# A hybrid decoder layer: norms of projection and down results dealt one token tile at a time, operands of the next products built in single steps

## The chip, the cores and the metric

The kernel runs on one core of a Trainium2 chip. The metric is the device time of one execution in microseconds (us), as the median of several runs. Beside the runs there is one profiled execution, from which every row below comes.

## The reference

One layer on 2048 tokens of width 1024, in float32. The first two lines below (projection, recurrent and attention heads) are far from the change; what matters is from `mix` on.

```python
u = rmsnorm(h, attn_pre_norm); proj = u @ w_in
o_hg, o_sb = ...                      # HGRN2 heads and stick-breaking heads, each normalised
mix = concatenate([o_hg, o_sb]) @ w_out
h = h + rmsnorm(mix, attn_post_norm)  # norm of the projection result
u = rmsnorm(h, ffn_pre_norm)
gate, up = split(u @ w_gate_up, [2816])
y = (silu(gate) * up) @ w_down
h = h + rmsnorm(y, ffn_post_norm)     # norm of the down result
h = h + (p @ ple_proj) * sigmoid(h @ ple_gate)
```

## The kernel before

Tokens are worked in four groups `g` of 512, each of four tiles of 128 rows. A float32 product is made on TensorE (PE) from three passes: an operand is split into a rounded high part (`uh`, `wh`) and the remainder (`ul`, `wl`), and `mm3` adds high by high, low by high and high by low (L221, L222, L223). The high part is a cast on ScalarE (ACT, L753), the low part a subtraction on VectorE (DVE) or GpSimd (POOL) (L754). `pair_of` (L745) makes both and is told which of the two engines subtracts: `V` is DVE, `G` is POOL.

After attention and recurrence come these stages:

- `out_proj(g)` (L611) multiplies by `w_out`; ACT (L643) and DVE (L645) bring its results into tiles `mix`. The projection of group 3 is the last and stands alone.
- `post_mix(g)` (L649) norms a group's projection result: for each token tile ACT squares (L258), POOL makes the reciprocal root (L260, L250, L252), DVE multiplies by root and gain (L660), POOL adds the residual (L661), the sum is squared and scaled in the same way, and both are stored (`h_s`, `un_s`).
- `turn` (L668) loads the normed rows, transposes them on PE and stores them as `u_s`, operands of the next product.
- Then a list of steps, run by `Drive`, two groups at a time: `gate_up(0)`, `down(0)`, `gate_up(1)`, `down(1)`, `ple(0)`, `ple(1)`. Each product of two matrices is cut into 2 by 2 blocks and made from seven block products in the order `CHAIN = (1, 2, 6, 3, 7, 5, 4)`, as in Strassen's scheme; sums and differences of blocks ("combos") are made on DVE or POOL before, and results are added together as they come (`chain`, L857). `gate_up` has 77 steps of 24 matmuls (11 blocks of the hidden width by seven products), `down` 77 steps of 12 matmuls (seven products by 11 blocks), each `ple` 36 steps.
- `t_first`, `t_second`, `t_all` build the token-side operands of the gate-and-up products from `u_s`; `s_all` and `s_one` those of the `ple` products from `h2t_s`. `post_y(g, i, ...)` (L1005) norms one token tile of a `down` result: it loads the gain twice and the residual twice, and stores two halves of `h2_s`, which a later `turn` transposes into `h2t_s`.

Loads by `load()` go out on SP's queue, all into one ring of ten tiles named `wr`, each 128 by 512 float32 (256 KB). A load is issued when the tile that it takes is free. `Drive.run` calls `prepare` of a step a fixed number of steps ahead of its matmuls: three in `gate_up` and `down`, five in `ple`. `at` and `spread` hook further work behind given steps. PE runs in the order of the program; on the other engines, and on SP, a scheduler puts the instructions in the order in which it takes them to be ready, and each engine then runs strictly in that order.

Of the kernel before, what the change touches and what calls it, by code (L numbers as in the profile page):

```python
# [18 lines left out]
ND = D // P  # L19
# [65 lines left out]
def hybrid_block(  # L85
# [563 lines left out]
    def post_mix(g, mix):  # L649
        gb = [ev(name="gb") for _ in range(2)]  # L650
        for j in range(2):
            nc.sync.dma_start(gb[j], attn_post_norm[0:1][:, j * GT:(j + 1) * GT].to_broadcast((P, GT)))
        for t in range(TT):
            hs = [xt("h"), xt("h")]
            for j in range(2):
                nc.sync.dma_start(hs[j], x[g * GT + t * P:g * GT + (t + 1) * P, j * GT:(j + 1) * GT])
            r = row_rstd(mix[t])
            for j in range(2):
                d = mix[t][j]
                nc.vector.scalar_tensor_tensor(d, d, r, gb[j], op0=ALU.mult, op1=ALU.mult)  # L660
                nc.gpsimd.tensor_tensor(hs[j], hs[j], d, op=ALU.add)  # L661
                nc.sync.dma_start(h_s[g][t * P:(t + 1) * P, j * GT:(j + 1) * GT], hs[j])
            r = row_rstd(hs)
            for j in range(2):
                nc.scalar.activation(mix[t][j], hs[j], AF.Copy, scale=r)
# [94 lines left out]
    def add(e, o, a, b):  # L760
        e.tensor_tensor(o, a, b, op=ALU.add)  # L761
# [33 lines left out]
    def t_blk(grp, i, j, k):  # L795
        return load(u_s[2 * grp + j][4 * i + k])
# [20 lines left out]

    def t_all(grp, tt, k):
        b11, b12, b21, b22 = (t_blk(grp, i, j, k) for i, j in ((0, 0), (0, 1), (1, 0), (1, 1)))
        for prod, b in ((1, b11), (2, b21), (3, b22)):  # L820
            tt[prod, k] = pair_of(b, "u", prod, V)
        b_combos(b11, b12, b21, b22, G)
        for prod, b in ((5, b11), (7, b12), (6, b22), (4, b21)):
            tt[prod, k] = pair_of(b, "u", prod, V)

    def s_blk(grp, i, j, k):
        return load(h2t_s[2 * grp + i][4 * j + k])

    def s_all(grp, ss, k):
        a11, a12, a21, a22 = (s_blk(grp, i, j, k) for i, j in ((0, 0), (0, 1), (1, 0), (1, 1)))  # L830
        for prod, a in ((1, a11), (2, a12), (4, a22)):
            ss[prod, k] = pair_of(a, "u", prod, V)
        add(G, a22, a21, a22)
        sub(G, a21, a11, a21)
        sub(G, a11, a22, a11)
        sub(G, a12, a12, a11)
        for prod, a in ((6, a11), (3, a12), (7, a21), (5, a22)):
            ss[prod, k] = pair_of(a, "u", prod, V)

    def s_one(grp, ss, prod, k):  # L840
        if prod in (1, 2, 4):
            a = s_blk(grp, *{1: (0, 0), 2: (0, 1), 4: (1, 1)}[prod], k)
        elif prod == 7:
            a, a21 = s_blk(grp, 0, 0, k), s_blk(grp, 1, 0, k)
            sub(V, a, a, a21)
        else:
            a21, a = s_blk(grp, 1, 0, k), s_blk(grp, 1, 1, k)
            add(V, a, a21, a)
            if prod != 5:
                a11 = s_blk(grp, 0, 0, k)  # L850
                sub(V, a, a, a11)
            if prod == 3:
                a12 = s_blk(grp, 0, 1, k)
                sub(V, a, a12, a)
        ss[prod, k] = pair_of(a, "u", prod, G)

    def chain(prod, c, b, new):  # L857

# [29 lines left out]
    def gate_up(grp, tt):  # L888
        def block(fb):
# [76 lines left out]
            blocks = blocks[2:]  # L966
        return steps + [b[p] for b in blocks for p in CHAIN]

    def down(grp):
        nfb = DFF // 256  # L970
        cs = [{} for _ in range(TT)]
# [2 lines left out]
        def product(n, prod):  # L974
# [12 lines left out]
            def run(k):  # L987
# [16 lines left out]
    def post_y(g, i, halves):  # L1004
# [151 lines left out]
    for g in range(NG - 1):  # L1156
# [5 lines left out]
            hgs[2].drain()  # L1162
            weave(op, OP_SLOTS - 6, rates.part(OP_SLOTS - 6), r3.part(OP_SLOTS - 6, 1))
        elif g == 1:
            weave(op, half, rates.part(half), r3.part(half, 1))
            tu = Stream(turn(un_s[0], u_s[0], g_ffn, "tr", xt, ev))
            weave(op, half, rates.part(half), r3.part(half, 1), (tu, 9, 0))
        else:
            weave(op, half, rates.part(half), r3.part(half, 1))
            hgs[3].drain()  # L1170
            att_stream.drain()
            side.close()
# [8 lines left out]
            for k in range(ND // 2):  # L1181
                t_first(0, tt0, 6, k)
        op.drain()
        post_mix(g, res[g]["mix"])
# [12 lines left out]

    def at(stage, step, f):
# [59 lines left out]
```

## Time and profile before

| quantity | value |
|---|---|
| time, median of 3 runs | 3174.49 us (3174.29 to 3177.37) |
| profiled execution: its own time | 3183.32 us |
| its span, first to last instruction | 3181.5 us |
| mean granted PE clock | 0.966 |
| busy share | PE 92%, DVE 63%, POOL 59%, ACT 50% |

Each row of a view is one group of instructions or one stretch of time. Busy shares are means over stages that differ. In rows of windows, the first number is the stretch, then its length, then busy time and count of instructions of each engine, then the granted PE clock (1.00 is full speed), the busy share of the 16 DMA engines and the GB/s that they moved. In rows of waits, the pair behind PE is what waited and what came last: total, times, longest, all in us.

### The profile page before, as it was taken

How to read it: one execution, taken by the hardware profiler on the slowest of the kernel's cores; microseconds unless marked ns; L12 is line 12 of the kernel's file. 1: busy time of each engine (PE TensorE's matmuls, PEld its weight loads, DVE VectorE, ACT ScalarE, POOL GpSimd, SP SyncE). 2: the span in 40 equal slices, each digit the busy share in tenths (PEclk: the TensorE clock that was granted, in tenths of full speed). 3: DMA queues.
4: the chain of work that ended last, by engine and by line, in shares of the span. 5: the costliest groups of instructions: out<-in, count | busy, mean ns of one | idle time of the engine just before them, and what ended most of it. 6: DMA issues, size and time to landing. Idle time of an engine off the chain costs nothing. (4 is left out here: it accounts for less than half of the span.)

```text
span 3181.5 us, 53147 instructions
## 1 busy us (share of the span) xinstructions
PE 2932.7 (92%) x18280; PEld 2455.3 (77%) x18280; DVE 1993.6 (63%) x2595; ACT 1591.3 (50%) x3187; POOL 1874.1 (59%) x1808
## 2 busy tenths in 40 slices
PE   7999899989999988778689999999799999998889
PEld 5888688868887877768568787878687888886667
DVE  3555566667776766555666666766575666655464
ACT  5666656656666665665433333355333332554342
POOL 3344445535556566665666666666756565766584
PEclk9999999999999999899789999999899999999989
DMA  6775465545545444548556676677755564677895
GB/s 186 221 209 164 135 182 162 152 131 163 160 147 156 128 141 132 169 142 287 183 187 209 229 239 219 210 218 230 265 181 178 193 211 149 210 217 252 283 317 163
DMA packets 467279, 613.32 MB, mean 193 GB/s; under 512 B 43840, under 2 KB 270144, under 8 KB 467008
## 3 DMA queue, kind: packets, MB, share of 16 engines
q1 hardware_dynamic: 467008, 609.92, 61.2%
q8 instruction: 144, 2.36, 0.3%
q14 instruction: 127, 1.04, 0.1%
HBM read 450.90 MB, written 158.86 MB: 192 GB/s over the span
## 5 line engine op out<-in xcount | busy, mean ns | idle before, releaser
L754 POOL TENSOR_TENSOR wl<-wr,wh 128x512 fp32r<-128x512 f32 x388 | 564.7, 1465 | 432.2 <-ACT wh L753 389.7
L753 ACT CAST wh<-wr 128x512 fp32r<-128x512 f32 x600 | 353.3, 620 | 565.7 <-PE mm L222 182.5
L413 POOL TENSOR_TENSOR a<-be,ring 128x512 f32<-128x512 f32 (+2 forms) x320 | 314.2, 982 | 493.9 <-DVE ring L409 462.7
L221 PE MATMUL mm<-uh,wh 128*128 128x512 f32 x1168 | 485.2, 415 | 2.2 <-DVE vv L328 1.9
L223 PE MATMUL mm<-uh,wl 128*128 128x512 f32 x1168 | 461.2, 395 | 0.0
L222 PE MATMUL mm<-ul,wh 128*128 128x512 f32 x1168 | 460.8, 394 | 0.0
L221 PE MATMUL mm<-wh,uh 128*128 128x256 f32 (+1 forms) x1024 | 322.0, 314 | 10.1 <-ACT mix L643 9.4
L754 DVE TENSOR_TENSOR wl<-wr,wh 128x512 fp32r<-128x512 f32 x212 | 222.7, 1062 | 166.1 <-ACT wh L753 153.3
L409 DVE TENSOR_TENSOR_SCAN ring<-z,ring,be 128x512 f32<-128x512 f32 x192 | 245.9, 1281 | 99.3 <-ACT z L395 94.0
L222 PE MATMUL mm<-wl,uh 128*128 128x256 f32 (+1 forms) x1024 | 305.1, 298 | 0.0
L223 PE MATMUL mm<-wh,ul 128*128 128x256 f32 (+1 forms) x1024 | 304.8, 298 | 0.0
L426 DVE TENSOR_TENSOR al<-tr,ah 128x512 fp32r<-128x512 f32 (+1 forms) x320 | 192.5, 601 | 113.4 <-ACT ah L424 112.4
L223 PEld LDWEIGHTS mm<-uh,wl 128*128 128x128 f32 x1168 | 221.9, 190 | 49.8
L221 PEld LDWEIGHTS mm<-uh,wh 128*128 128x128 f32 x1168 | 223.5, 191 | 43.8 <-issue 2.0
L207 ACT CAST wh<-wr 128x512 fp32r<-128x512 f32 x288 | 178.4, 620 | 150.3 <-PE mm L222 75.3
L222 PEld LDWEIGHTS mm<-ul,wh 128*128 128x128 f32 x1168 | 223.2, 191 | 38.9
L208 POOL TENSOR_TENSOR wl<-wr,wh 128x512 fp32r<-128x512 f32 x144 | 187.7, 1303 | 84.1 <-ACT wh L207 74.7
L394 ACT ACTIVATE be<-z 128x512 f32<-128x512 f32 (+2 forms) x320 | 171.3, 535 | 101.8 <-PE z L388 50.0
L424 ACT CAST ah<-tr 128x512 fp32r<-128x512 f32 (+1 forms) x320 | 167.7, 524 | 94.9 <-PE tr L421 91.4
L221 PEld LDWEIGHTS mm<-wh,uh 128*128 128x128 f32 x1024 | 200.8, 196 | 18.4 <-ACT mix L643 10.1
L222 PEld LDWEIGHTS mm<-wl,uh 128*128 128x128 f32 x1024 | 201.1, 196 | 5.2
L223 PEld LDWEIGHTS mm<-wh,ul 128*128 128x128 f32 x1024 | 200.5, 196 | 3.9
(288 smaller groups left out, 7363.5 us busy)
## 6 DMA issues: line engine op xcount, KB each, us to landing
wr<-in_w_gate_up_dram SPq DMA_DIRECT2D x308, 256.0 KB, 3.4
wr<-in_w_in_dram SPq DMA_DIRECT2D x224, 256.0 KB, 3.2
wr<-hid_s SPq DMA_DIRECT2D x154, 256.0 KB, 3.6
wr<-in_w_down_dram SPq DMA_DIRECT2D x110, 256.0 KB, 3.2
wr<-h_s SPq DMA_DIRECT2D x96, 256.0 KB, 4.2
hid_s<-hs SPq DMA_DIRECT2D x88, 256.0 KB, 2.9
wr<-wd_s SPq DMA_DIRECT2D x88, 256.0 KB, 4.1
kt<-k_s SPq DMA_DIRECT2D x80, 256.0 KB, 3.0
```

What stands on the lines that cost most here:

```text
L207: nc.scalar.copy(hi, src)
L208: (lo_engine or nc.gpsimd).tensor_tensor(lo, src, hi.bitcast(F32), op=ALU.subtract)
L221: nc.tensor.matmul(o, l[0], r[0], start=start, stop=False)
L222: nc.tensor.matmul(o, l[0], r[1], start=False, stop=False)
L223: nc.tensor.matmul(o, l[1], r[0], start=False, stop=stop)
L394: nc.scalar.activation(be[:, :n], z[:, :n], AF.Sigmoid, scale=0.125)
L409: nc.vector.tensor_tensor_scan(r[:, o:o + n][:, ::-1], z[:, :n][:, ::-1], be[:, :n][:, ::-1], init, op0=ALU.mult, op1=ALU.bypass)
L413: nc.gpsimd.tensor_tensor(a[:, :n], be[:, :n], r[:, o + 1:o + n + 1], op=ALU.mult)
L424: nc.scalar.copy(hi[:, lo_c:], tr[:, lo_c:])
L426: nc.vector.tensor_tensor(lo[:, lo_c:], tr[:, lo_c:], hi[:, lo_c:].bitcast(F32), op=ALU.subtract)
L753: nc.scalar.copy(hi, src)
L754: lo_engine.tensor_tensor(lo, src, hi.bitcast(F32), op=ALU.subtract)
```

## The change

Eight edits, which leave every matmul as it is:

1. `post_mix` yields behind each token tile. Those of groups 0 to 2 are woven into the next `out_proj`, one tile at a time; that of group 3 goes behind steps 0 to 3 of `gate_up(0)`, one tile each (before: all four behind step 0).
2. Behind the last `out_proj`, `prepare` runs for four steps (before: for two, ahead of that `out_proj`, as still now); the four calls of `t_second` are hooked behind steps 0 to 3 of `gate_up(0)` (before: all ahead of step 0).
3. `down` prepares four steps ahead, not three.
4. `post_y` is called per tile behind steps 67, 69, 71 and 73 of `down`, or 0 to 3 of the stage that follows (before: four tiles at once behind products 5 and 4).
5. `t_all` and `s_all` are generators, spread over nine steps for each `k`; their combos go from POOL to DVE.
6. `s_one`, one product per step with its own loads (56 in all), becomes `s_part`, two parts for each `k`, with 32 loads.
7. In `gate_up` DVE makes the low parts of the second tile of every product, and both of products 6 and 3 (before: the second tile of products 2 and 7 alone).
8. The turns of groups 2 and 3 in `ple(0)` start one step later.

```diff
@@ post_mix
                 nc.sync.dma_start(un_s[g][t * P:(t + 1) * P, j * GT:(j + 1) * GT], mix[t][j])
+            yield
@@ t_all (s_all in the same way, add and sub from G to V)
         b11, b12, b21, b22 = (t_blk(grp, i, j, k) for i, j in ((0, 0), (0, 1), (1, 0), (1, 1)))
+        yield
         for prod, b in ((1, b11), (2, b21), (3, b22)):
             tt[prod, k] = pair_of(b, "u", prod, V)
-        b_combos(b11, b12, b21, b22, G)
+            yield
+        b_combos(b11, b12, b21, b22, V)
...
-    def s_one(grp, ss, prod, k):
...
-        ss[prod, k] = pair_of(a, "u", prod, G)
+    def s_part(grp, ss, part, k):
+
+        a11, a12, a21, a22 = (s_blk(grp, i, j, k) for i, j in ((0, 0), (0, 1), (1, 0), (1, 1)))
+        if part == 0:
+            ss[1, k] = pair_of(a11, "u", 1, G)
+            ss[2, k] = pair_of(a12, "u", 2, V)
+            add(V, a21, a21, a22)
+            sub(V, a21, a21, a11)
+            ss[6, k] = pair_of(a21, "u", 6, V)
         else:
+            ss[4, k] = pair_of(a22, "u", 4, G)
+            add(V, a22, a21, a22)
+            sub(V, a21, a11, a21)
+            sub(V, a11, a22, a11)
+            sub(V, a12, a12, a11)
+            for prod, a, e in ((3, a12, V), (7, a21, V), (5, a22, G)):
+                ss[prod, k] = pair_of(a, "u", prod, e)
@@ gate_up, prepare
-                s[prod] = [pair_of(t, "w", prod, V if n and prod in (2, 7) else G) for n, t in enumerate(w)]
+                s[prod] = [pair_of(t, "w", prod, V if n or prod in (6, 3) else G) for n, t in enumerate(w)]
@@ down, run
                 if k == nfb - 1 and prod in (5, 4):
-                    for i in range(TT):
-                        half = 0 if prod == 5 else 1
-                        post_y(2 * grp + half, i, [cs[i][1 + half, 1], cs[i][1 + half, 2]])
+                    half = 0 if prod == 5 else 1
+                    ready[2 * grp + half] = [[cs[i][1 + half, 1], cs[i][1 + half, 2]] for i in range(TT)]
@@ the last projection and the steps
-    drive = Drive([(gate_up(0, tt0), 3), (down(0), 3), (gate_up(1, tt1), 3), (down(1), 3),
+        pm = Stream(post_mix(g, res[g]["mix"]))
+
+    drive = Drive([(gate_up(0, tt0), 3), (down(0), 4), (gate_up(1, tt1), 3), (down(1), 4),
                    (ple(0, ss0), 5), (ple(1, ss1), 5)])
     drive.prepare(2)
-    Stream(out_proj(NG - 1, res[NG - 1])).drain()
+    op = Stream(out_proj(NG - 1, res[NG - 1]))
+    weave(op, OP_SLOTS, (pm, TT, 0))
+    op.drain()
...
-    for k in range(ND // 2):
-        t_second(0, tt0, k)
-
+    drive.prepare(4)
...
-    at(0, 0, lambda: post_mix(NG - 1, res[NG - 1]["mix"]))
+    for k in range(ND // 2):
+        at(0, k, lambda k=k: t_second(0, tt0, k))
+    spread(0, 0, post_mix(NG - 1, res[NG - 1]["mix"]), TT)
...
-        at(1, 6 + 15 * k, lambda k=k: t_all(1, tt1, k))
+        spread(1, 3 + 18 * k, t_all(1, tt1, k), 9, 2)
         at(2, 10 + 16 * k, lambda k=k: ple_combos(k))
-        at(3, 6 + 15 * k, lambda k=k: s_all(0, ss0, k))
+        spread(3, 3 + 18 * k, s_all(0, ss0, k), 9, 2)
+    for g in range(NG):
+        stage, step = ((1, 67), (2, 0), (3, 67), (4, 0))[g]
+        for i in range(TT):
+            at(stage, step + (2 * i if g % 2 == 0 else i), lambda g=g, i=i: post_y(g, i))
...
-        spread(4, 1 + 9 * i, turner(h2_s[g], h2t_s[g], None), 9)
-    for i, prod in enumerate(CHAIN):
+        spread(4, 2 + 9 * i, turner(h2_s[g], h2t_s[g], None), 9)
+    for i in range(2):
         for k in range(ND // 2):
-            n = 12 + 4 * i + k
-            at(4 + n // 36, n % 36, lambda prod=prod, k=k: s_one(1, ss1, prod, k))
+            at(4, 21 + 7 * i + 2 * k - i * k, lambda i=i, k=k: s_part(1, ss1, i, k))
```

Two places where the order of instructions moves are shown. The first is ACT's order where the last `out_proj` ends and `gate_up(0)` begins. `mix` is the last projection result, `uh` a token-side operand of `t_second`, `wh` a weight operand of a later step, `cu` the copy of the first block product. Before:

```order
L643 ACTIVATE mix<-mm,rg 128x256 x2
L258 ACTIVATE junk,ss<-mix 128x512
L753 CAST uh<-wr 128x512 x8
L861 COPY cu<-mm 128x512
L753 CAST uh<-wr 128x512
L861 COPY cu<-z 128x512
L753 CAST uh<-wr 128x512 x7
L753 CAST wh<-wr 128x512 x6
L258 ACTIVATE junk,ss<-h 128x512 x2
```

And with the change:

```order
L643 ACTIVATE mix<-mm,rg 128x256 x2
L258 ACTIVATE junk,ss<-mix 128x512
L754 CAST wh<-wr 128x512 x2
L754 CAST uh<-wr 128x512 x4
L754 CAST wh<-wr 128x512
L869 COPY cu<-mm 128x512
L754 CAST wh<-wr 128x512 x2
L869 COPY cu<-z 128x512
L754 CAST uh<-wr 128x512 x4
L754 CAST wh<-wr 128x512
L258 ACTIVATE junk,ss<-h 128x512 x2
```

Before, all 16 `uh` of `t_second` stand ahead of the first further weights; now the weights of steps 2 to 4 stand between eight of them, and the other eight follow later.

The second is SP's order in the last product of `down(0)`, where the loads of `post_y` for group 0 stand (gain `ffn_post_norm`, residual `h_s0`, results to `h2_s0`), beside the loads of the product (`hid_s0`, `wd_s`). Before, with the last of sixteen `post_y` loads and the first loads of the product behind them:

```order
L738 DMA wr_26009<-in_ffn_post_norm_dram 128x512
L738 DMA wr_26012<-h_s0_87 128x512
L1012 DMA h2_s0_91<-c12_25322 128x512
L738 DMA wr_26016<-in_ffn_post_norm_dram 128x512
L738 DMA wr_26019<-h_s0_87 128x512
L1012 DMA h2_s0_91<-c11_24699 128x512
L738 DMA wr_26023<-hid_s0_111 128x512
L738 DMA wr_26025<-wd_s3_278 128x512
L738 DMA wr_26051<-hid_s0_111 128x512
```

And with the change, from the second of the four tiles:

```order
L739 DMA wr_26071<-in_ffn_post_norm_dram 128x512
L739 DMA wr_26074<-h_s0_87 128x512
L1022 DMA h2_s0_91<-c11_24706 128x512
L739 DMA wr_26078<-in_ffn_post_norm_dram 128x512
L739 DMA wr_26081<-h_s0_87 128x512
L1022 DMA h2_s0_91<-c12_25306 128x512
L739 DMA wr_26085<-hid_s0_111 128x512
L739 DMA wr_26087<-wd_s8_283 128x512
L739 DMA wr_26109<-hid_s0_111 128x512
L739 DMA wr_26111<-wd_s9_284 128x512
L739 DMA wr_26146<-in_ffn_post_norm_dram 128x512
```

Before, all sixteen `post_y` loads stand ahead of the product's fourth block (`wd_s3`); now four of them alternate with four loads of the product, from its fifth block or later on.

Up to the end of the second-last `out_proj`, ACT, DVE and POOL have the same order in both kernels, row for row, though `post_mix` of groups 0 and 1 is written into the loop in another way. PE's order is the same throughout but for two sets of four transposes, one step later. DVE has 198 instructions more, POOL 202 fewer, SP 24 fewer (the loads that `s_part` saves).

More of the change, by code (lines that the diff above doesn't have):

```diff
@@ L830, in s_all @@
         a11, a12, a21, a22 = (s_blk(grp, i, j, k) for i, j in ((0, 0), (0, 1), (1, 0), (1, 1)))
+        yield
         for prod, a in ((1, a11), (2, a12), (4, a22)):
             ss[prod, k] = pair_of(a, "u", prod, V)
[L833 to L836, printed above, removed]
+            yield
+        add(V, a22, a21, a22)
+        sub(V, a21, a11, a21)
+        sub(V, a11, a22, a11)
+        sub(V, a12, a12, a11)
         for prod, a in ((6, a11), (3, a12), (7, a21), (5, a22)):
             ss[prod, k] = pair_of(a, "u", prod, V)
-    def s_one(grp, ss, prod, k):
[L841 to L845, printed above, removed]
-        else:
[L847 to L854, printed above, removed]
-        ss[prod, k] = pair_of(a, "u", prod, G)
+            yield
+    def s_part(grp, ss, part, k):
[6 more added lines that the diff above has]
+            ss[6, k] = pair_of(a21, "u", 6, V)
+        else:
+            ss[4, k] = pair_of(a22, "u", 4, G)
+            add(V, a22, a21, a22)
+            sub(V, a21, a11, a21)
+            sub(V, a11, a22, a11)
+            sub(V, a12, a12, a11)
+            for prod, a, e in ((3, a12, V), (7, a21, V), (5, a22, G)):
+                ss[prod, k] = pair_of(a, "u", prod, e)
     def chain(prod, c, b, new):
@@ L967, in gate_up @@
         return steps + [b[p] for b in blocks for p in CHAIN]
+    ready = {}
     def down(grp):
@@ L995, in run, with post_y @@
                 if k == nfb - 1 and prod in (5, 4):
-                    for i in range(TT):
-                        half = 0 if prod == 5 else 1
-                        post_y(2 * grp + half, i, [cs[i][1 + half, 1], cs[i][1 + half, 2]])
+                    half = 0 if prod == 5 else 1
+                    ready[2 * grp + half] = [[cs[i][1 + half, 1], cs[i][1 + half, 2]] for i in range(TT)]
             return [(lambda k=k: prepare(k), lambda k=k: run(k)) for k in range(nfb)]
         return [st for n, prod in enumerate(CHAIN) for st in product(n, prod)]
-    def post_y(g, i, halves):
+    def post_y(g, i):
+        halves = ready[g][i]
         r = row_rstd(halves)
@@ L1164, in hybrid_block @@
         elif g == 1:
-            weave(op, half, rates.part(half), r3.part(half, 1))
+            weave(op, half, rates.part(half), r3.part(half, 1), (pm, TT, 0))
             tu = Stream(turn(un_s[0], u_s[0], g_ffn, "tr", xt, ev))
@@ L1168, in hybrid_block @@
         else:
-            weave(op, half, rates.part(half), r3.part(half, 1))
+            weave(op, half, rates.part(half), r3.part(half, 1), (pm, TT, 0))
             hgs[3].drain()
@@ L1183, in hybrid_block @@
         op.drain()
-        post_mix(g, res[g]["mix"])
-    drive = Drive([(gate_up(0, tt0), 3), (down(0), 3), (gate_up(1, tt1), 3), (down(1), 3),
+        pm = Stream(post_mix(g, res[g]["mix"]))
+    drive = Drive([(gate_up(0, tt0), 3), (down(0), 4), (gate_up(1, tt1), 3), (down(1), 4),
                    (ple(0, ss0), 5), (ple(1, ss1), 5)])
     drive.prepare(2)
-    Stream(out_proj(NG - 1, res[NG - 1])).drain()
+    op = Stream(out_proj(NG - 1, res[NG - 1]))
+    weave(op, OP_SLOTS, (pm, TT, 0))
+    op.drain()
     wpool_open.close()
```

1 line of the change is left out of this document (added).

## The prediction

> **What bounds the kernel now.** I read the engines' busy shares first:
>
> ```profile
> span 3181.5 us, 53147 instructions
> PE 2932.7 (92%) x18280; PEld 2455.3 (77%) x18280; DVE 1993.6 (63%) x2595; ACT 1591.3 (50%) x3187; POOL 1874.1 (59%) x1808
> ```
>
> PE sets the time and its matmuls do not change. So the question is where PE idles, and where its clock is halved, within reach of the edits. I read the stretches next (length, busy PE, PEld, DVE, ACT, POOL, clock, DMA share, GB/s):
>
> ```profile
> 1553.00:1625.00 72.00, 42.04 (x144) 31.10 (x143) 45.89 (x52) 35.22 (x74) 49.88 (x52) 0.72 0.69 219
> 1625.00:2010.00 385.00, 373.84 (x1671) 308.52 (x1670) 258.33 (x318) 121.25 (x211) 241.32 (x167) 0.98 0.67 218
> 2225.00:2300.00 75.00, 56.99 (x223) 44.93 (x222) 44.01 (x50) 28.74 (x62) 61.08 (x60) 0.84 0.82 274
> 2300.00:2690.00 390.00, 386.55 (x1726) 319.21 (x1726) 265.67 (x326) 125.67 (x215) 238.29 (x167) 0.99 0.57 185
> 2690.00:2890.00 200.00, 200.00 (x884) 165.42 (x883) 116.96 (x132) 98.54 (x177) 134.65 (x90) 1.00 0.67 210
> 2890.00:2960.00 70.00, 49.40 (x194) 39.29 (x193) 35.85 (x42) 28.54 (x61) 51.54 (x54) 0.83 0.81 269
> 2960.00:3100.00 140.00, 123.10 (x543) 99.16 (x542) 79.22 (x95) 60.16 (x106) 87.52 (x62) 0.93 0.89 298
> ```
>
> The fifth stretch runs at full clock without a gap: 200.00/884 = 0.226 us for a matmul. By that pace the 144 matmuls of the first stretch need 32.6 of its 72 us, so 39.4 are lost; the stretch at 2225 loses 75 − 50.4 = 24.6, at 2890 70 − 43.9 = 26.1, at 2960 140 − 122.8 = 17.2 (a little more, since some of these are short transposes). The loss is idle time plus clock: at 1553, 30 us idle (72 − 42.04) and 9 of slower matmuls, with the clock at 0.72. The whole gate-and-up stretches (1625, 2300) lose hardly anything.
>
> Then PE's waits, for the stretches from 1240, 1640, 2230, 2330 and 2910 us in this order:
>
> ```profile
> PE tr L221 <- ACT wh L753: 13.3, 1, 13.3
> PE av L221 <- ACT wh L753: 12.6, 2, 7.4
> PE mm L221 <- ACT mix L643: 9.4, 2, 8.3
> PE hg L503 <- POOL qp L540: 8.8, 2, 5.9
> PE tr L223 <- POOL wl L754: 3.7, 1, 3.7
> ...
> PE z L223 <- DVE wl L754: 1.0, 1, 1.0
> ...
> PE z L221 <- ACT wh L753: 14.7, 2, 10.2
> ...
> PE tr L223 <- POOL wl L754: 3.5, 1, 3.5
> ...
> PE z L221 <- ACT wh L753: 14.2, 2, 10.8
> PE hg L687 <- DMA wr<-h_s: 9.3, 2, 7.2
> ```
>
> The long waits are for a cast of weights on ACT, one kind at four places. What makes ACT late differs. At 2242 and 2909 on ACT, and for the first of them on SP:
>
> ```profile
> 2242.42 1.95 ACT L753 CAST wh<-wr 128x512 fp32r<-128x512 f32 x3 [12.68 <-DMA wr<-hid_s]
> ...
> 2909.74 1.94 ACT L753 CAST wh<-wr 128x512 fp32r<-128x512 f32 x3 [13.23 <-DMA wr<-hid_s]
> ...
> 2212.97 0.33 SPq L738 DMA_DIRECT2D wr<-in_ffn_post_norm_dram  x1
> ...
> 2235.27 0.45 SPq L738 DMA_DIRECT2D wr<-h_s  x1
> 2236.42 0.42 SPq L738 DMA_DIRECT2D wr<-hid_s  x1
> ```
>
> From 2212.97 to 2235.27 SP issues the sixteen loads of `post_y`; the product's next load stands behind them and goes out at 2236.42. The wait before 2909 is the same burst of group 2. At 1564 ACT is late by its order instead: its casts of weights stand behind sixteen `uh` casts of `t_second`, which wait for DVE (its idle time of 4.26 us ends with DVE's last combo):
>
> ```profile
> 1576.98 3.22 ACT L753 CAST wh<-wr 128x512 fp32r<-128x512 f32 x6 [4.26 <-DVE wr L758]
> ```
>
> **The change part by part.** The durations (count, then total us and mean ns) by group, two single operations of one form on DVE, and ACT in the last projection:
>
> ```profile
> L754 POOL TENSOR_TENSOR wl<-wr,wh 128x512 fp32r<-128x512 f32 x388 | 564.7, 1465 | 432.2 <-ACT wh L753 389.7
> L754 DVE TENSOR_TENSOR wl<-wr,wh 128x512 fp32r<-128x512 f32 x212 | 222.7, 1062 | 166.1 <-ACT wh L753 153.3
> L761 DVE TENSOR_TENSOR c<-mm,cu 128x512 f32<-128x512 f32 x74 | 50.0, 684 | 40.5 <-PE mm L223 40.1 <-DMA un_s<-mix 0.4
> ...
> 1590.44 1.78 DVE L758 TENSOR_TENSOR wr<-wr 128x512 f32<-128x512 f32 x1
> 1609.46 0.69 DVE L758 TENSOR_TENSOR wr<-wr 128x512 f32<-128x512 f32 x1
> ...
> 1521.48 1.34 ACT L665 ACTIVATE mix<-h,rstd 128x512 f32<-128x512 f32 x2 [3.16 <-POOL rstd L252]
> ```
>
> *Weaving `post_mix`* (1): groups 0 and 1 leave the engines' orders as they were, so the waits there (POOL `qp`, 8.8 us) stay: 0. In the last projection, PE's 8.3 us wait for ACT `mix` ends with ACT behind L665, which waits for POOL's root; there POOL now has one `wl` (1.465 us) fewer ahead. Gain 1.5, bounds 0 and 5.
>
> *`prepare(4)` and the dealt `t_second`* (2), between 1553 and 1625: weights for step 2 are cast ahead, and the 13.3 and 3.7 us go. What is late next is step 5 (product 6 of the second block), whose second operand DVE reaches as its 43rd instruction after the projection, behind combos of `t_second`, L660 and `chain` adds. DVE takes 45.89/52 = 0.88 us each here, so 38 us from 1553, that is 1591; by the 1.062 us of the `wl` row, 1599. PE, at 5.5 us (24 × 0.226) a step, wants it at 1553 + 27.5 + 1.4 = 1582. So 9 to 17 us of wait. DVE's waits for loads come on top of its busy time, so I take 16, with 6 for the clock (as 9 go with 30 now): 22 of the 39.4 stay, gain 17. Bounds: 35 (DVE slips in ahead) and 5 (those waits are as long as now, when 26 of DVE's 72 us are idle).
>
> *`post_y` by tiles, lead of four* (3, 4): sixteen loads and eight stores of 256 KB no longer stand in a row, yet they remain. From the start of the last product to the next stage the queue carries 14 loads of the product, 10 for `gate_up(1)`, 16 and 8 for `post_y`: 48 transfers, 12.6 MB. The stretch at 2960 has 298 GB/s at a DMA share of 0.89, so 335 at full share: 37.6 us, against 11 steps of 12 × 0.226 = 2.7, that is 30 us. So about 7.7 us of the wait stay, in pieces, and 1.4 for the clock: of 24.6 lost, 15.5 gained. Bounds 6 (as many pieces again) and 23. The group 2 burst (2890 to 2960) is alike, 7 kept; in addition the turn's wait of 9.3 us for `h_s` loads behind `post_y(3)` goes to some 3 with eight loads fewer ahead of it and a start one step later: 26.1 − 7 − 3 − 3 for clock = 13. Bounds 3 and 22.
>
> The Trainium skill, "DMA: Bandwidth & Descriptors", section "Where 436 GB/s comes from", says that transfers between HBM and SBUF are bound by the HBM side at about 358 GB/s per core. By that 12.6 MB would take 35.2 us, 5.2 kept instead of 7.7, an estimate from the page that the 335 here neither reaches nor contradicts.
>
> *Low parts to DVE* (7): seven more of the 14 in each of 22 blocks. At 1.062 us 77 more are 82 us in 390 us of `gate_up(1)`: DVE goes from 266 to 347, 89%; POOL falls by 77 × 1.465 = 113 to 126. The add with one operand outside SBUF takes 0.684, so 0.38 of the 1.062 is meeting POOL, which will be met half as often: DVE then nearer 76%. Hidden by the lead of three steps (16 us); without that cover each late low part costs its own microsecond. I set a loss of 3, bounds 0 and 26 (at the 1.78 us of the slower single one: 77 × 1.78 + 266 = 403, 13 over, twice). The 3.5 us wait for POOL `wl` at 2447, behind POOL's sums, goes: gain 3.5, bounds 0 and 5.
>
> The Trainium skill, "SBUF — State Buffer", section "SBUF: two separate sides", says that a DVE operation with two SBUF inputs and a GpSimd one that reads SBUF take the shared ports as an exclusive lock, each for its whole instruction. The two single durations, 1.78 and 0.69 us, agree with it; by that rule each moved subtraction holds the lock for 0.69 us where POOL held it for up to 1.465, and the move would leave no loss at all.
>
> *`t_all`, `s_all`* (5) lie in the `down` stages, where PE has no gap (2690: 200.00 of 200.00 us) and DVE 117 of 200 us: sixteen combos per stage added there are 17 us, 0. *`s_part`* (6): 24 loads fewer are 6.3 MB, 19 us at 335 GB/s, in a stretch at DMA share 0.89; against it steps 28 to 31 each give DVE four sums and two subtractions, 4 × 0.9 + 2 × 1.06 = 5.7 us in 2.7 of matmuls, ten steps or so ahead of most use. Of the 17.2 lost I take half as staying, since steps on DVE replace loads: gain 8, bounds −5 and 15.
>
> **Sum:** 1.5 + 17 + 15.5 + 13 + 3.5 + 8 − 3 = 55.5. The profiled execution took 3183.3 us (span 3181.5 and 1.8 around it), so 3127.8 by its own measure; the median of the runs is 8.8 lower than it, so 3174.5 − 55.5 = 3119.
>
> **Rivals.** *Half of it* (moved waits): the bytes remain and the queue is the same; the waits break up but sum to the same where DMA is at 0.8 to 0.9, and step 5 waits as long as step 2 did. Then 3.5, 5, 6, 3 and 8 are left, 25: 3149. For it speaks that the share is already 0.82 in the burst; against, that the stretch before had room (0.67 at 2690). *All of it*: the losses above vanish, 39.4 + 24.6 + 26.1 + 17.2 and 3.5 for `wl`, 111, of which 20 stay for the DMA: 3084. *Slower: DVE late in each block.* DVE now holds combos, both low parts of product 6, and the adds from PE, strictly in order; if an add waits for PE and the low parts stand behind it, PE waits in every block. At 4 us in each of 22 blocks (2.7 idle, the rest clock) 88 go against 55: 3207. It decides from 2.5 us a block. The waits of only 1.0 for DVE `wl` in 385 us speak against it; its 67% there become 76 to 89. *Nothing*: the order written by hand is undone by the scheduler, as for groups 0 and 1: 3174; ACT's and SP's orders as quoted speak against it.
>
> **How the numbers follow.** Forecast 3119: 0.56 (its own range 3095 to 3142). Half of it: 0.17. All of it: 0.13. Slower: 0.09. Nothing: 0.05. The range of eight in ten goes from 3079, five below the case of all of it, to 3160, ten above that of half. Faster by over 0.2% (6.3 us, about what runs of this kernel tell apart) holds the first three, 0.86; within it 0.05, slower 0.09.
>
> **What would show it.** Step 2 of `gate_up(0)` without a wait and a later one of 9 to 17 us for DVE `wl` or ACT `wh` near 1582 to 1600. No ACT idle of 12 us for `hid_s` at the last products of `down`; waits under 4 us there. DVE at 76% in `gate_up(1)`, its `wl` mean below 1.06. Waits of 1 us or more for DVE in most blocks would make the forecast wrong upward; a clean start of `gate_up(0)` would make it wrong downward.

## The result and the profile after

The changed kernel takes 3140.09 us (median of 4 runs, 3137.09 to 3140.98) against 3175.38 us of the kernel before (4 runs, 3174.29 to 3177.37). The ratio is 0.9886, 95% interval 0.9869 to 0.9904: 35 us or 1.1% faster, where 55.5 had been forecast (3119, range 3079 to 3160). The profiled execution took 3140.98 us, 42.3 less than that of before. The page of the changed kernel, and its stretches that answer to those shown of before (columns as there), with one more inside `down(0)`, from 2050:

```profile
span 3139.2 us, 52948 instructions
PE 2927.5 (93%) x18280; PEld 2455.3 (78%) x18280; DVE 2030.1 (65%) x2793; ACT 1587.0 (51%) x3187; POOL 1622.3 (52%) x1606
...
1553.00:1625.00 72.00, 59.00 (x257) 47.12 (x256) 54.88 (x69) 37.69 (x79) 49.64 (x46) 0.91 0.63 208
1625.00:2010.00 385.00, 372.46 (x1661) 307.16 (x1660) 278.09 (x395) 122.22 (x213) 171.22 (x109) 0.98 0.70 227
2050.00:2200.00 150.00, 150.00 (x664) 124.20 (x663) 83.30 (x105) 77.03 (x137) 80.35 (x57) 1.00 0.73 224
2195.00:2270.00 75.00, 67.46 (x286) 54.37 (x285) 55.37 (x64) 33.38 (x71) 59.55 (x58) 0.95 0.83 284
2270.00:2660.00 390.00, 388.30 (x1742) 320.80 (x1741) 279.10 (x399) 126.12 (x215) 157.58 (x98) 1.00 0.59 190
2660.00:2850.00 190.00, 189.89 (x838) 156.91 (x837) 116.85 (x142) 96.71 (x174) 104.60 (x71) 1.00 0.68 215
2850.00:2920.00 70.00, 58.27 (x238) 46.43 (x237) 40.97 (x45) 31.67 (x69) 55.95 (x55) 0.88 0.90 309
2920.00:3060.00 140.00, 119.92 (x509) 95.41 (x509) 93.32 (x106) 58.68 (x103) 70.80 (x48) 0.90 0.74 245
```

The start of `gate_up(0)` (1553) does 257 matmuls in the 72 us in which it did 144, with the clock at 0.91 and not 0.72; the end of `down(0)` (2195) 286 in 75 us, not 223. The last row is the exception: 119.92 us of PE in 140, where it was 123.10, and a clock of 0.90 for 0.93. The waits of PE in the changed kernel, in the stretches from 1550, 1640, 2190, 2290, 2840 and 2930 us:

```profile
PE av L221 <- ACT wh L754: 5.6, 1, 5.6
PE av L223 <- DVE wl L755: 4.6, 2, 3.2
PE mm L221 <- DVE c L762: 2.7, 2, 1.8
...
PE hg L712 <- ACT pt L715: 6.5, 1, 6.5
PE hg L688 <- ACT acc L694: 6.1, 2, 4.2
...
PE tr L223 <- DVE wl L755: 5.2, 1, 5.2
PE mm L223 <- POOL wl L755: 1.6, 1, 1.6
...
PE tr L223 <- DVE wl L755: 1.2, 1, 1.2
...
PE hg L688 <- DMA wr<-h_s: 11.3, 2, 7.6
...
PE mm L221 <- ACT wh L754: 6.8, 2, 5.0
PE z L222 <- POOL wl L755: 5.1, 1, 5.1
PE z L221 <- ACT wh L754: 3.6, 1, 3.6
```

The waits of 13.3, 10.2 and 10.8 us for a cast are gone. The turn's wait for its loads has grown from 9.3 to 11.3, and the last stretch still has its waits for `wh` and `wl`.

**Where the 42 us lie.** PE runs nearly the same instructions in the same order in all these kernels, so the time between two of them, counted from the first, measures a stretch. I cut the program at ten points that way. The columns are named by the times at which the stretch stands in the first trace of before; only the columns at the turn differ a little in what they hold, since its transposes move by steps. Each entry is from one profiled execution, in us, and the rows from the fourth on are the experiments.

| kernel | to 1509 | 1509–1717 last projection, start of `gate_up(0)` | 1717–2073 | 2073–2308 end of `down(0)` | 2308–2457 | 2457–2742 | 2742–2939 end of `down(1)` | 2939–2975 turn | 2975–3056 | 3056–3104 start of `ple(1)` | rest |
|---|---|---|---|---|---|---|---|---|---|---|---|
| before | 1490.7 | 208.3 | 355.4 | 235.6 | 148.7 | 285.3 | 196.4 | 36.5 | 81.2 | 47.2 | 77.9 |
| before, again | 1494.5 | 206.0 | 354.4 | 236.1 | 149.0 | 286.0 | 195.9 | 36.4 | 80.2 | 45.6 | 77.9 |
| the change | 1494.8 | 193.4 | 347.4 | 219.1 | 144.9 | 286.2 | 182.1 | 42.1 | 79.2 | 55.3 | 77.9 |
| edit 2 alone | 1487.0 | 210.9 | 351.9 | 235.5 | 148.7 | 285.4 | 194.8 | 35.5 | 79.5 | 45.8 | 77.9 |
| edit 7 alone | 1486.5 | 203.3 | 348.5 | 232.9 | 145.4 | 286.6 | 195.6 | 37.5 | 79.1 | 47.0 | 77.9 |
| change, edit 7 undone | 1487.7 | 203.9 | 350.6 | 219.4 | 150.1 | 286.1 | 182.5 | 41.0 | 79.3 | 55.1 | 78.0 |
| change, `post_mix(3)` one burst | 1492.5 | 195.7 | 349.1 | 218.8 | 145.0 | 286.4 | 182.1 | 40.5 | 78.8 | 54.9 | 77.9 |
| change, edit 4 undone | 1490.3 | 193.7 | 346.3 | 231.7 | 147.5 | 286.2 | 194.5 | 34.9 | 77.6 | 57.1 | 77.9 |
| change, edit 3 undone | 1495.3 | 190.5 | 352.1 | 217.0 | 144.7 | 288.4 | 185.7 | 38.5 | 76.6 | 57.1 | 77.9 |
| change, edit 6 undone | 1493.9 | 191.5 | 348.6 | 219.2 | 147.5 | 286.5 | 182.3 | 40.8 | 78.8 | 45.8 | 77.9 |
| change, parts of `s_part` later | 1494.4 | 189.9 | 351.1 | 217.0 | 144.8 | 286.1 | 182.0 | 40.7 | 78.4 | 37.1 | 92.1 |
| change, turns later | 1484.1 | 192.8 | 348.1 | 217.7 | 144.4 | 286.5 | 182.4 | 40.1 | 75.1 | 57.0 | 77.9 |
| change, gain loaded once | 1489.8 | 190.6 | 351.0 | 219.8 | 146.2 | 287.1 | 185.4 | 35.1 | 78.6 | 55.5 | 77.8 |
| three repairs | 1488.3 | 192.7 | 347.8 | 219.6 | 147.4 | 286.3 | 185.4 | 32.0 | 75.1 | 50.2 | 77.8 |

The first column is the same work in the same order in all of them and spreads from 1484.1 to 1495.3. Total times of single executions are therefore worth no more than some 10 us here. The later columns repeat within some 3 us where the code is alike, and the experiments are read from those. The exceptions are the two columns up to 2073: a turn's wait for ACT falls now before and now behind the cut at 1717, and the second of them goes from 346.3 to 352.1 in traces with the same code. Their sum repeats: the change and the seven traces with its `gate_up(0)` have 540.1 to 542.6.

Against the mean of the two traces of before, the change gains 21.3 us at the start of and in `gate_up(0)` (562.1 to 540.8), 16.8 at the end of `down(0)`, 4.0 after it, 14.1 at the end of `down(1)`; it loses 5.7 at the turn, gains 1.5 in the rest of `ple(0)`, and loses 8.9 at the start of `ple(1)`.

The stretch from 1509 to 2073, cut at steps of `gate_up(0)` in the same way:

| kernel | 1509 to step 0 | steps 0 to 2 | steps 3 to 8 | step 9 to 2073 |
|---|---|---|---|---|
| before | 44.3 | 38.4 | 50.7 | 430.3 |
| before, again | 42.4 | 38.0 | 50.6 | 429.3 |
| the change | 44.9 | 16.3 | 50.1 | 429.5 |
| seven more with its `gate_up(0)` | 45.2–47.3 | 16.3 | 49.8–54.1 | 426.3–429.5 |
| edit 2 alone | 45.0 | 16.3 | 69.0 | 432.4 |
| edit 7 alone | 42.8 | 32.4 | 53.1 | 423.4 |
| change, edit 7 undone | 46.4 | 16.3 | 66.2 | 425.5 |
| change, `post_mix(3)` one burst | 45.2 | 16.3 | 58.5 | 424.8 |

The gain of the change lies in steps 0 to 2, and every trace with edit 2 has it. Whether it is kept is decided in steps 3 to 8.

### The profile page after: what moved, and what is told of

Its sections match the earlier page's. It is cut to its first block, busy times and chain, and to the rows that moved or that the text cites. A ratio compares the mean times of both kernels' runs of the same rounds, so it can differ in the third digit from the quotient of the medians.

```text
span 3139.2 us, 52948 instructions
## 1 busy us (share of the span) xinstructions
PE 2927.5 (93%) x18280; PEld 2455.3 (78%) x18280; DVE 2030.1 (65%) x2793; ACT 1587.0 (51%) x3187; POOL 1622.3 (52%) x1606
## 5 line engine op out<-in xcount | busy, mean ns | idle before, releaser
L755 POOL TENSOR_TENSOR wl<-wr,wh 128x512 fp32r<-128x512 f32 x256 | 370.4, 1454 | 360.9 <-ACT wh L754 343.6
L755 DVE TENSOR_TENSOR wl<-wr,wh 128x512 fp32r<-128x512 f32 x344 | 313.0, 915 | 178.9 <-ACT wh L754 163.0
L207 ACT CAST wh<-wr 128x512 fp32r<-128x512 f32 x288 | 177.9, 618 | 151.9 <-PE mm L222 79.2
L208 POOL TENSOR_TENSOR wl<-wr,wh 128x512 fp32r<-128x512 f32 x144 | 187.5, 1302 | 84.1 <-ACT wh L207 78.9
```

What stands on the lines that cost most here:

```text
L207: nc.scalar.copy(hi, src)
L208: (lo_engine or nc.gpsimd).tensor_tensor(lo, src, hi.bitcast(F32), op=ALU.subtract)
L755: lo_engine.tensor_tensor(lo, src, hi.bitcast(F32), op=ALU.subtract)
```

## The experiments

**The kernel before once more**, unchanged.

> The kernel before, unchanged, profiled a second time. The profiled execution of before took 3183.3 us, 8 above the median of its runs (3175.4), that of the change 0.9 above its median (3140.1), so the two traces differ by 42.3 us and the medians by 35.3. Theory: the 8 us belong to that one execution and lie in one or two places, so a second trace takes about 3175 and differs from the first by some 7 to 8 us, at a place that can be named. Rival: they are the profiler's and come again, about 3183.

3181.9 us, the rival's number. The theory fell: the second trace is not 7 to 8 us shorter. It runs behind the first by up to 6.6 us inside the untouched stretch and ends 1.4 us ahead of it. Whether profiling itself makes this kernel longer, as the rival has it, stays open: the two profiled executions of before stand at 3183.3 and 3181.9, and other runs of the same kernel beside these experiments lay between 3170.6 and 3183.0. What makes the untouched stretch longer or shorter stays open too.

**Edit 2 alone**, on the kernel before.

```diff
-    for k in range(ND // 2):
-        t_second(0, tt0, k)
+    drive.prepare(4)
...
+    for k in range(ND // 2):
+        at(0, k, lambda k=k: t_second(0, tt0, k))
```

> The kernel before with edit 2 alone: prepare for four steps behind the last projection and t_second behind steps 0 to 3; post_mix of group 3 stays one burst behind step 0. Theory: edit 2 alone makes the gain at the start of gate_up(0), where the two traces part by 23 us between 1505 and 2070: the 13.3 us wait at step 2 goes, a wait of 9 to 17 us in step 5 stays, and the time is about 3175 - 20 = 3155. Rival: dealing post_mix by tiles is needed as well, since its burst stands ahead of the operands of step 5 on DVE and ACT: a gain of 10 or less, 3165 or more.

3172.2 us; 562.8 us from the last projection to 2073, before 563.7 and 560.4: nothing gained in sum. Steps 0 to 2 take 16.3 us, 22 less than before, and steps 3 to 8 take 69.0, 18 more. PE's waits between 1550 and 1640:

```profile
PE av L221 <- ACT wh L753: 25.3, 2, 13.7
PE mm L221 <- DVE c L761: 4.5, 1, 4.5
```

Step 2's wait is gone, and two of 13.7 and 11.6 us stand in its place, both in step 5, one for each of its two tiles of weights. The rival was right that this edit needs another, but which one the next runs tell.

**Edit 7 undone**, and **edit 7 alone** on the kernel before (the same line the other way).

```diff
-                s[prod] = [pair_of(t, "w", prod, V if n or prod in (6, 3) else G) for n, t in enumerate(w)]
+                s[prod] = [pair_of(t, "w", prod, V if n and prod in (2, 7) else G) for n, t in enumerate(w)]
```

> The change with edit 7 undone: low parts of the gate-and-up weights on POOL but for the second tile of products 2 and 7. Theory: they are hidden on either engine, but POOL holds them behind its sums of hid: only the wait of 3.5 us for POOL wl in gate_up(1) comes back, about 3144, with DVE back from 76 to 67 per cent of gate_up(1). Rival: DVE with more to do makes the turns and casts of gate_up(0) late (waits of 4.2 and 5.2 us are new there), so that undoing it gains: 3135.

> The kernel before with edit 7 alone: DVE makes the low parts of the second tile of every gate-and-up product and both of products 6 and 3. From the last projection to the end of gate_up(0) the kernel before takes 563 and 560 us, edit 2 alone 563, the change without edit 7 554, the change 541. Theory: the parts add, and edit 7 alone is worth the 13 us that the change loses without it: 549, and with 4 to 5 us for POOL's wait in gate_up(1) a time of 3182 - 18 = 3164. Rival: edit 7 works only where edit 2 has opened the way; alone, with the sixteen casts of t_second ahead of the weights and DVE loaded more, it gains nothing there or loses: 560 or more, 3175.

Without edit 7 the change takes 3151.5 us: 13.7 are lost up to 2073 (554.5 for 540.8) and 5.2 in the column at 2308, where POOL's wait comes back (4.1 us). Steps 3 to 8 take 66.2 us for 50.1, nearly as long as with edit 2 alone. Alone on the kernel before, edit 7 takes 3158.7: 551.8 up to 2073, 10 gained, and 3.5 at 2308. None of the 10 is in steps 3 to 8; some 6 lie in steps 0 to 2, and some 6 behind step 8, where the turn's wait is shorter. That wait before, and with edit 7 alone:

```profile
PE hg L687 <- ACT acc L693: 6.0, 1, 6.0
...
PE hg L687 <- ACT acc L693: 2.2, 2, 1.8
```

The waits for this turn also move between traces with the same code (3.3 to 8.4 us in sum), so the second 6 are not shown to be edit 7's. In the first of the two runs both theories fell, since neither had the loss up to 2073; in the second the theory was nearer in number, though the parts do not add as it says.

What edit 7 does to DVE and POOL stands in the busy times. With edit 7 alone, DVE's low parts by group, then a row of 390 us inside `gate_up(1)` that begins at the same matmul as the row of before at 2300 (busy times in the order PE, PEld, DVE, ACT, POOL):

```profile
L754 DVE TENSOR_TENSOR wl<-wr,wh 128x512 fp32r<-128x512 f32 x344 | 331.2, 972 | 162.0 <-ACT wh L753 147.3 <-PE mm L222 6.1 <-PE z L222 4.1
...
2280.00:2670.00 390.00, 387.00 (x1736) 319.90 (x1735) 279.93 (x397) 126.97 (x216) 155.13 (x98) 1.00 0.57 185
```

The same group in the change:

```profile
L755 DVE TENSOR_TENSOR wl<-wr,wh 128x512 fp32r<-128x512 f32 x344 | 313.0, 915 | 178.9 <-ACT wh L754 163.0 <-PE z L222 8.1 <-PE mm L222 4.1
```

Against before (265.67 us for 326 on DVE, 238.29 for 167 on POOL), edit 7 alone has 71 more operations on DVE for 14.3 us more, and 69 fewer on POOL for 83.2 us less. A moved subtraction costs DVE 0.20 us net; the prediction had 1.06 without relief, and 0.4 with it (76% of 390 us). The others on DVE become shorter as POOL meets them less often: the mean of a low part there falls from 1062 to 972 ns, and to 915 in the change, while the sums with one operand outside SBUF (`c<-mm,cu`) stay at 684. The Trainium skill, "SBUF — State Buffer", section "SBUF: two separate sides", says of the port pair that DVE and GpSimd share that one of the two holds it for a whole instruction and the other waits. The sum of the two engines' times, 69 us less here, fits that.

What waits PE has without edit 7, between 1550 and 1640:

```profile
PE mm L221 <- DVE c L762: 14.2, 2, 7.2
PE av L221 <- ACT wh L754: 5.4, 1, 5.4
PE mm L222 <- POOL ul L755: 2.6, 1, 2.6
```

The wait of 7.2 us ends at 1624.4. Ahead of the sum `c` that ends it, DVE does and waits as follows; the last row is what SP's loads waited for, from 1560 to 1622:

```profile
1602.37 3.44 DVE L759 TENSOR_TENSOR wr<-wr 128x512 f32<-128x512 f32 x2
1605.73 3.43 DVE L755 TENSOR_TENSOR ul<-wr,uh 128x512 fp32r<-128x512 f32 x2
1619.98 0.79 DVE L759 TENSOR_TENSOR wr<-wr 128x512 f32<-128x512 f32 x1 [9.13 <-DMA wr<-in_w_down_dram]
...
SPq L739 <- DVE ul L755: 12.1, 6, 5.8
```

DVE's operations take 1.7 us each here, beside a POOL that works without a gap from 1596.8 to 1617.0. SP's loads wait for tiles that DVE still reads, and DVE then stands 9.13 us for a load of `w_down`, ahead of the sum that PE needs. So the low parts themselves are not what is late: the order on DVE and the ring of tiles carry the delay on. That this chain is all of the 13.7 us is not shown.

**`post_mix` of the last group as one burst.**

```diff
-    spread(0, 0, post_mix(NG - 1, res[NG - 1]["mix"]), TT)
+    at(0, 0, lambda: Stream(post_mix(NG - 1, res[NG - 1]["mix"])).drain())
```

> The change with one part of edit 1 undone: post_mix of the last group as one burst behind step 0 of gate_up(0). From the last projection to the end of gate_up(0) the kernel before takes 563 and 560 us, the change 541; edit 2 alone takes 563, and the change without edit 7 554, so neither part makes the gain by itself. Theory: edit 7 and the dealing of post_mix share it, as both shorten what stands ahead of step 5's and step 7's operands: the burst alone costs some 8, 549 and a time of 3148. Rival: edit 7 on top of edit 2 is all of it, and the dealing does nothing: 541 to 543.

3141.4 us; 544.8 up to 2073, 4 more than the change. At the place itself the dealing is worth more: steps 3 to 8 take 58.5 us, 8.4 more than in the change, and PE waits 19.1 us for `wh` against 5.6. Half of that comes back behind step 8 (424.8 us for 429.5). The theory's 8 us hold for these steps, the rival is nearer in the sum.

**Edit 4 undone**: `post_y` in bursts, the lead of four kept.

```diff
-        stage, step = ((1, 67), (2, 0), (3, 67), (4, 0))[g]
         for i in range(TT):
-            at(stage, step + (2 * i if g % 2 == 0 else i), lambda g=g, i=i: post_y(g, i))
+            at(1 if g < 2 else 3, 65 if g % 2 == 0 else 76, lambda g=g, i=i: post_y(g, i))
```

> The change with edit 4 undone: post_y for four tiles at once behind the last step of products 5 and 4 of down, as before; the lead of four steps stays. Theory: dealing post_y is what took away the waits of 10 to 11 us at the start of the last product of down, so both come back and with them some 15 us each: about 3140 + 30 = 3170. Rival: the longer lead covers the burst, since SP issues the product's loads a step sooner: 3140 + 10 = 3150 or less.

3156.1 us. The last products of `down` lose 12.6 and 12.4 us (231.7 for 219.1, 194.5 for 182.1), and 7.2 come back at the turn (34.9 for 42.1). Between 2190 and 2290, and on ACT there:

```profile
PE z L221 <- ACT wh L754: 11.5, 2, 7.7
...
2214.82 1.31 ACT L754 CAST wh<-wr 128x512 fp32r<-128x512 f32 x2 [11.96 <-DMA wr<-hid_s]
```

The wait for `hid_s` behind the burst is back on ACT, nearly as long as before (11.96 us, it was 12.68). The theory holds for the two bursts in the last products. It lacked that the dealing of the last group costs 7 us at the turn.

**Edit 3 undone**: a lead of three.

```diff
-    drive = Drive([(gate_up(0, tt0), 3), (down(0), 4), (gate_up(1, tt1), 3), (down(1), 4),
+    drive = Drive([(gate_up(0, tt0), 3), (down(0), 3), (gate_up(1, tt1), 3), (down(1), 3),
```

> The change with edit 3 undone: down prepares three steps ahead, not four. Theory: the lead matters only in the last product, where post_y's loads share the queue: one step of 2.7 us at each of the two places, with clock, 3140 + 8 = 3148. Rival: it does nothing once post_y is dealt: 3140.

3142.7 us. The end of `down(0)` is 2.1 us shorter, that of `down(1)` 3.6 longer with the turn 3.6 shorter; nothing in sum, as the rival had it.

**Edit 6 undone**: `s_one` as before in place of `s_part`.

```diff
-            at(4, 21 + 7 * i + 2 * k - i * k, lambda i=i, k=k: s_part(1, ss1, i, k))
+            n = 12 + 4 * i + k
+            at(4 + n // 36, n % 36, lambda prod=prod, k=k: s_one(1, ss1, prod, k))
```

> The change with edit 6 undone: s_one with its 56 loads, one product a step, in place of s_part with 32. Between ple(0)'s last steps and the first of ple(1) the change is 8 us slower against the kernel before, where I had forecast 8 faster. Theory: s_part does this, since its four-tile groups hold four of the ten wr tiles until DVE's chain of sums is through, and the next weights are loaded behind them: undoing it gains some 8, about 3132. Rival: s_part only stands where the loads dealt from post_y and the later turn have pushed the work, and 24 loads more make it worse: 3140 to 3150.

3132.2 us; the start of `ple(1)` takes 45.8 us, as before the change (47.2 and 45.6), not 55.3. So `s_part`, with its 24 loads fewer, is what costs 9 there. In the change, on SP and then on ACT:

```profile
3005.61 3.56 SPq L739 DMA_DIRECT2D wr<-h2t_s  x4
3009.53 0.34 SPq L1067 DMA_DIRECT2D out_dram<-c  x1
3009.92 0.42 SPq L739 DMA_DIRECT2D wr<-in_ple_gate_dram  x1
3012.02 0.34 SPq L1067 DMA_DIRECT2D out_dram<-c  x1
3012.41 5.96 SPq L739 DMA_DIRECT2D wr<-in_ple_gate_dram  x3
...
3013.58 0.62 ACT L754 CAST wh<-wr 128x512 fp32r<-128x512 f32 x1 [6.63 <-DMA wr<-in_ple_gate_dram]
3016.69 2.18 ACT L754 CAST uh<-wr 128x512 fp32r<-128x512 f32 x4 [0.55 <-DVE wr L759]
```

The weights of a product of `ple(1)` go out behind four loads of a part, over 6 us for three of them, and ACT casts a part's four operands in between, when DVE has their sums. With `s_one` the same four loads of weights leave within 3 us:

```profile
3005.77 0.33 SPq L739 DMA_DIRECT2D wr<-in_ple_gate_dram  x1
...
3006.86 1.59 SPq L739 DMA_DIRECT2D wr<-in_ple_gate_dram  x3
```

That `s_part` costs the 9 us is shown; that it does so by this order on SP and ACT is read from these rows.

**The second parts of `s_part` later**, and between.

```diff
-    for i in range(2):
-        for k in range(ND // 2):
-            at(4, 21 + 7 * i + 2 * k - i * k, lambda i=i, k=k: s_part(1, ss1, i, k))
+    for k in range(ND // 2):
+        at(4, 21 + 2 * k, lambda k=k: s_part(1, ss1, 0, k))
+        at(5, 2 * k, lambda k=k: s_part(1, ss1, 1, k))
```

> The change with the second parts of s_part moved from steps 28 to 31 of ple(0) to steps 0, 2, 4 and 6 of ple(1); their products are wanted from step 12 of ple(1) on. Theory: the waits of 1.8, 1.7, 3.6 and 5.1 us at the start of ple(1) come of loads of weights that stand behind those parts' loads, with the ring of ten tiles held; they go, and the time is 3140 - 10 = 3130. Rival: DVE and POOL, both with the adds of the last products there, are what is late, and the parts only come later: within 3 us of 3140.

3132.0 us. The start of `ple(1)` falls to 37.1 us, 18 below the change and 9 below the kernel before. So the waits there come with the parts, and are not those of DVE's and POOL's adds alone. But 14 come back later, with one wait:

```profile
PE mm L221 <- ACT uh L754: 10.0, 2, 9.5
```

The parts are now late for their own product. The sum fits the forecast (8 against 10), the reason only half.

**The turns two steps later.**

```diff
-        spread(4, 2 + 9 * i, turner(h2_s[g], h2t_s[g], None), 9)
+        spread(4, 4 + 9 * i, turner(h2_s[g], h2t_s[g], None), 9)
```

> The change with the turns of groups 2 and 3 in ple(0) two steps later still (from steps 4 and 13). Theory: the turn's waits for its loads (7.6 and 3.7 us) come of the sixteen loads of post_y(3) that share SP's queue and the ring in steps 0 to 3; two steps, 5.4 us, and a half-clock stretch are won: 3140 - 8 = 3132. Rival: the loads of the turn are slow by themselves and wait wherever they stand, or the operands built from them come later by as much: 3140 or more.

3124.9 us, of which 10.7 are the untouched first stretch. In `ple(0)` 2.0 and 4.1 are gained, and 1.7 lost at the start of `ple(1)`. The turn's wait is not shorter, it is one and not two:

```profile
PE hg L688 <- DMA wr<-h_s: 11.9, 2, 11.2
```

Inconclusive on the cause of the wait: the gain has the size of the theory (6 for 8), the wait that of the rival.

**The gain of the norm loaded once**, 30 loads of 256 KB fewer.

```diff
+    gys = []
     def post_y(g, i):
+        if not gys:
+            for j in range(2):
+                gys.append(big[1].tile([P, GT], F32, tag="gy", name="gy", bufs=2))
+                nc.sync.dma_start(gys[j], ffn_post_norm[0:1][:, j * GT:(j + 1) * GT].to_broadcast((P, GT)))
...
-            gy = load(ffn_post_norm[0:1][:, cs].to_broadcast((P, GT)))
+            gy = gys[j]
```

> The change with the gain of the down norm loaded once, into two tiles of its own, and not twice for every token tile: 30 loads of 256 KB fewer, 8 fewer at each of the four places where post_y stands (two remain at the first). Theory: at the start of ple(0) the turn waits for its loads (7.6 and 3.7 us) because post_y(3)'s sixteen loads share the ring of ten tiles and SP's queue; with eight the two waits fall to 5 in sum, and each last product of down (219 and 182 us stretches) loses another 3: 3140 - 12 = 3128. Rival: the turn waits because post_y's own stores and the norm's chain on ACT, POOL and DVE are late, or because its loads are slow; fewer loads do nothing: 3138 or more.

3136.2 us. Here the cause shows: the turn takes 35.1 us for 42.1, and its wait for loads falls by half.

```profile
PE hg L688 <- DMA wr<-h_s: 5.5, 2, 4.2
PE hg L688 <- ACT acc L692: 3.0, 2, 2.2
```

So the turn's loads wait behind those of `post_y(3)`. The other half of the expectation failed: the last products of `down` gain nothing (219.8 and 185.4 for 219.1 and 182.1). With half of `post_y`'s loads gone there, fewer bytes did not shorten what is left of their wait. What is, I did not find out; a wait of 2.4 us for a POOL `wl` at the start of the last product is new in this kernel.

**Three repairs together**: the gain once, the turns two steps later, the second parts at steps 32 and 34 of `ple(0)` and 0 and 2 of `ple(1)`.

```diff
+    for k, n in enumerate((32, 34, 36, 38)):
+        at(4 + n // 36, n % 36, lambda k=k: s_part(1, ss1, 1, k))
```

> Three repairs of the change together: the gain loaded once, the turns in ple(0) two steps later, and the second parts of s_part at steps 32 and 34 of ple(0) and 0 and 2 of ple(1), between the change's (28 to 31, where the next weights' loads stood behind theirs) and the late ones (0 to 6 of ple(1), where a wait of 9.5 us for a cast uh came at product 3). Theory: each place is a wait of its own, so that they add: 12 from the gains, 6 from the turns, 12 from the parts, less some 5 that two of them share: 3140 - 25 = 3115. Rival: the stretch of the two ple stages is bound by bytes, and what one repair frees the next wait takes: 3125 or more.

3122.8 us (median of 4 runs, 3120.4 to 3128.0) against 3178.3 of the kernel before on the same chip (7 runs): ratio 0.9829, interval 0.9813 to 0.9846. The interval lies wholly below that of the change (0.9869 to 0.9904), so this version beats both kernels. Its gains in the stretches: turn 10.1 and 4.1, start of `ple(1)` 5.1, against losses of 2.5 in the column at 2308 and 3.3 at the end of `down(1)`: 13 where 25 had been expected. The time lies between the theory's 3115 and the rival's 3125. PE's longest waits from 2840 on:

```profile
PE av L222 <- POOL wl L755: 4.3, 2, 3.4
PE z L222 <- DVE wl L755: 4.3, 2, 2.3
PE hg L688 <- DMA wr<-h_s: 3.6, 2, 2.1
```

The turn is cured. At the start of `ple(1)` low parts on POOL and DVE are what is late now, where casts and loads were.

## Why the prediction was right, and where it was off

The direction and the range held. By its steps:

- **Weaving `post_mix`: 1.5.** For groups 0 and 1 right: the untouched stretch is 1494.8 us, within that stretch's spread. The wait for `mix` in the last projection went from 8.3 to 5.4, by 3 and not 1.5, and edit 7 makes that (4.8 with edit 7 alone, 7.8 in the change without it). But the projection became no shorter (44.9 us up to step 0, for 44.3 and 42.4), since waits of 3.6 and 3.3 us for low parts on DVE stand there now, where one of 2.0 stood.
- **`prepare(4)` and the dealt `t_second`: 17.** Steps 0 to 8 take 66.4 us where they took 88.9: 22 gained. The reasoning held for what is late: step 2's waits are gone, and of 12.9 us of waits that stay, 10.2 are in step 5, for a cast on ACT and low parts on DVE (forecast 16 there). What it lacked is a condition. The 22 us are there with edit 2 alone, but steps 3 to 8 then lose 18 of them; they lose 16 in the change without edit 7, and 8 without the dealing of `post_mix`. The change without edit 2 was not run; but steps 0 to 2 take 16.3 us in the eleven traces with edit 2, and 32.4 to 38.4 in the three without.
- **Low parts to DVE: −3.** The step that failed. Apart from POOL's wait at 2447, the prediction weighed only what DVE would lose, and counted the relief as a smaller loss. Undoing this edit costs 13.7 us up to 2073. DVE was forecast at 76% of `gate_up(1)` and stood at 72 (279.10 of 390 us); a moved subtraction cost it 0.20 us net, and POOL was freed of 1.2 us each.
- **POOL's wait at 2447: 3.5.** Measured 4.0, and edit 7 makes it: it comes back without it.
- **`post_y` in the last products: 15.5, and the larger part of the second place's 13.** Right: 16.8 and 14.1 were measured, and undoing the dealing takes some 12.5 of each. The 7 us that I kept at each place for bytes are not shown to be that: with half the loads nothing of them went.
- **`t_all` and `s_all`: 0.** No run undoes this edit alone. Where they stand PE has no gap in the change: 150.00 of 150 us from 2050, 189.89 of 190 from 2660.
- **The turn's wait, 9.3 to 3: failed.** It grew to 11.3. I counted loads ahead of the turn and left out that dealing puts the rest of them beside its own: 5.7 us lost where 6 were to be won, and 7.2 come back when the dealing is undone.
- **`s_part`: +8, measured −9.** The term with the wrong sign. I counted bytes saved (19 us of transfer) in a stretch that I took as bound by bytes. What cost time there were the parts: by the rows, four loads of a part ahead of the next weights on SP, and their casts on ACT. Two of the four waits there stand in the kernel before as well (3.4 and 4.0 us, now 3.6 and 5.1). The bound of −5 that I had set was too narrow.
- **The baseline.** I carried the 8.8 us by which the profiled run of before lay above its median over to the change. There it was 0.9. That is 8 of the 20 us between 55.5 and 35.3. The other 13 lie between the sum and the traces (42.3): 17 at `s_part` and 3 at the end of `down(1)` with the turn, less the 7 by which the other terms gave more than forecast.

Of the rivals, "half of it" came nearest in size (25), though not by its mechanism: at the bursts the waits went. "DVE late in each block" is ruled out: between 2290 and 2650, some nine blocks, PE waited 1.2 us for a DVE `wl`.

## What to carry to other kernels

Where two engines slow each other, price a moved operation by the sum of both engines' times, not by its own duration: what the others gain can be more than it costs. An edit that takes one wait away may show no gain until the next wait is gone too, so cut the stretch at its steps and not only at its end. Dealing a burst of loads out takes away the wait behind it, but count what stands beside each piece in its new place, in the same queue and the same ring of tiles. And saving bytes helps only where bytes are late: look first at which order puts the next operand behind the work that is moved.

## What was not expected of the hardware

Moving some 70 subtractions of 128 by 512 float32 from GpSimd to VectorE made VectorE's time grow by 14.3 us and GpSimd's fall by 83.2, in 390 us. The first 1490 us, with the same order of instructions on the compute engines, took between 1484.1 and 1495.3 us in fourteen executions.
